# Where the sums, silus and splits of seven-product weight pairs stand in the engine queues

## The chip, the cores and the metric

One core of a Trainium2 chip runs the whole program in one launch. The metric is device time in microseconds (us); lower is better. All data is float32. Products run on TensorE (PE) as three float32r matmuls each: every operand is split into a high part and a remainder, and hi*hi, hi*lo and lo*hi are accumulated.

## The reference

A network of two blocks on 512 tokens of width 1024. What this change touches is the gated feed-forward layer of the second block, which is computed four times:

```python
def _swiglu(h, w_gu, w_down):
    gate, up = jnp.split(h @ w_gu, 2, axis=-1)
    return (jax.nn.silu(gate) * up) @ w_down

def second_block(x, ...):
    for l in range(DEPTH):                                  # DEPTH = 2
        x = _layer_norm(alpha * x + 0.5 * _swiglu(x, ffn_w_gu[l, 0], ffn_w_down[l, 0]), ...)
        mix = _token_mixers(x, ...)
        x = _layer_norm(alpha * x + mix, ...)
        x = _layer_norm(alpha * x + 0.5 * _swiglu(x, ffn_w_gu[l, 1], ffn_w_down[l, 1]), ...)
    return x
```

The hidden width is 2816, that is 22 chunks of 128 columns for the gate and 22 for the up half.

## The kernel before

A scheduling layer turns the program into one in-order queue per engine: PE, VectorE (DVE), ScalarE (ACT), GpSimd (POOL), and SyncE (SP), which issues every load. The scheduler may reorder, so the code's order is not quite the queue's; `tc.issue_after(ins)` keeps an instruction behind another one in its queue. An instruction that waits holds up everything behind it in its queue.

In `swiglu` (L1116) the hidden chunks are computed in three parts (8, 8 and 6 chunks), each followed by products with the down weights (`we`). The first four or five chunks of a layer go through `plain`. The others, 71 in all, go through `gated` (L1011): a chunk of gate weights and the chunk of up weights are a **pair**, and a 2 x 2 block product of the pair (gate and up weights split along the contraction, the operand split along contraction and tokens) is formed with seven products in place of eight. Seven-product pairs stand in twelve runs: one of 3 pairs, three of 4, four of 8 and four of 6.

A pair needs, in the order of the PE queue, the products named `11`, `12`, `p2`, `p1`, `p3`, `22` and `p4`, each of 12 matmuls on 256 columns. The products `22` and `p4` of a pair come one pair late: the loop in `swiglu` interleaves the generators, so that PE does 11(k), 12(k), 22(k-1), p2(k), p1(k), p4(k-1), p3(k), and then the next pair.

The weights come from `strassen_w` (L972). Two loads per pair, `ra` (tile wr, three buffers, L448) and `rb` (tile wr2, two buffers, L991); then four sums of 128 x 512 on POOL: p1 = a21 + a22 (L995), p2 = p1 + a11 (L996), p3 = a11 + a21 (L998), p4 = p2 + a12 (L999); then splits. A split is a copy on ACT that makes the high part (L472) and a subtraction on DVE that makes the remainder (L473). A pair has four weight splits: (11, 12) and (p2, p1), which share the buffers wh and wl, and (p3, p4), all of 128 x 1024, and (22) of 128 x 512.

The partial sums of the three products that share the PSUM tile R are copied out by ACT: e1 (L1028) after `11`, e2 (L1037) after `p2`, e3 (L1043) after `p3`. Since R goes on accumulating, PE may not start `p2` before e1, `p3` before e2, nor `22` before e3 is done. DVE adds what is left: g1 (L1032), g1 times up (L1051), g2 (L1054), n2 (L1045), the product with g2 (L1056). Two silus on ACT (L1023), and a split of the finished 128 x 512 chunk (tiles ph, pl).

Before a run of pairs the operand is prepared: `Strassen.combine` (L337) makes four sums of 128 x 256 on POOL for each of four operand blocks (L342 to L345) and splits them. That happens four times in the program, while `plain` runs.

Of the kernel before, what the change touches and what calls it, by code (L numbers as in the profile page):

```python
# [13 lines left out]
ALU = mybir.AluOpType  # L14
# [7 lines left out]
H = T // 2  # L22
# [280 lines left out]
class Strassen:  # L303
# [33 lines left out]
    def combine(self, j, x):  # L337
        nc, p = self.p.nc, self.p
        b11, b12, b21, b22 = (x[k][:, c] for k in (j, j + 4) for c in HALVES)
        raw = p.pool.tile([P, 2 * T], F32, tag="wc", name=p.nm("wc"), bufs=2)  # L340
        d, t3, t4, f = (raw[:, i * H : i * H + H] for i in range(4))
        nc.gpsimd.tensor_tensor(t3, b22, b12, op=ALU.subtract)  # L342
        nc.gpsimd.tensor_tensor(f, t3, b11, op=ALU.add)
        nc.gpsimd.tensor_tensor(d, b11, b12, op=ALU.subtract)
        nc.gpsimd.tensor_tensor(t4, f, b21, op=ALU.subtract)  # L345
        hi, lo = self.place(j, 3)
        nc.scalar.activation(hi, f, AF.Copy, scale=-1.0)
        nc.vector.scalar_tensor_tensor(
            out=lo, in0=f, scalar=-1.0, in1=hi.bitcast(F32), op0=ALU.mult, op1=ALU.subtract
        )  # L350
        for i, n in ((0, 2), (2, 1)) if j == 0 else ((0, 3),):
            p.split(raw[:, i * H : (i + n) * H], *self.place(j, i, n))


class Prog:
# [156 lines left out]

    def mac(self, W, X, cols=slice(0, T), tag=None, off=None):

# [452 lines left out]

        return X1, scale, X, finish

    def strassen_w(self, sa, sb, behind):  # L970


        nc = self.nc
        out = {}

        def put(names, src, tags, bufs=2, pool=None, behind=()):
            n = len(names) * 512
            hi, lo = ((pool or self.pool).tile([P, n], F32R, tag=t, name=self.nm(t), bufs=bufs) for t in tags)
            with ExitStack() as ctx:
                for ins in behind:  # L980
                    ctx.enter_context(self.tc.issue_after(ins))
                self.split(src, hi[:], lo[:])
            for i, name in enumerate(names):
                out[name] = [
                    (hi[:, c : c + P], lo[:, c : c + P]) for c in range(i * 512, i * 512 + 512, P)
                ]

        ra = self.raw(sa, 1024)
        put(("11", "12"), ra[:], ("wh", "wl"), pool=self.main)
        rb = self.pool.tile([P, 1024], F32, tag="wr2", name=self.nm("wr2"), bufs=2)  # L990
        nc.sync.dma_start(rb[:], sb)  # L991
        a11, a12, a21, a22 = ra[:, :512], ra[:, 512:], rb[:, :512], rb[:, 512:]
        c1, c2 = (self.pool.tile([P, 1024], F32, tag="wc", name=self.nm("wc"), bufs=2) for _ in range(2))
        p2, p1, p3, p4 = c1[:, :512], c1[:, 512:], c2[:, :512], c2[:, 512:]
        nc.gpsimd.tensor_tensor(p1, a21, a22, op=ALU.add)  # L995
        nc.gpsimd.tensor_tensor(p2, p1, a11, op=ALU.add)  # L996
        put(("p2", "p1"), c1[:], ("wh", "wl"), pool=self.main, behind=behind[0])
        nc.gpsimd.tensor_tensor(p3, a11, a21, op=ALU.add)  # L998
        nc.gpsimd.tensor_tensor(p4, p2, a12, op=ALU.add)  # L999
        put(("p3", "p4"), c2[:], ("wh2", "wl2"), behind=behind[1])  # L1000
        put(("22",), a22, ("wh3", "wl3"), 1)
        return out

    def prod(self, ps, W, X, start):

# [7 lines left out]
    def gated(self, X, srcs, mid, tags):  # L1013

        nc = self.nc
        tr, tq, tz = tags  # L1020
        gv, hv = self.scratch()
        g1, g2, e1, n2 = gv[:, :H], gv[:, H:], hv[:, :H], hv[:, H:]
        silu = lambda t: nc.scalar.activation(t, t, AF.Silu)  # L1023
        W = self.strassen_w(*srcs, self.behind)
        self.behind = behind = [[], []]
        R = self.pt(tag=next(tr))
        self.prod(R, W["11"], X["11"], True)
        nc.scalar.copy(e1, R[:, :H])  # L1028
        yield
        Z = self.pt(tag=next(tz))  # L1030
        self.prod(Z, W["12"], X["21"], True)
        behind[0].append(nc.vector.tensor_tensor(g1, e1, Z[:, :H], op=ALU.add).ins)  # L1032
        silu(g1)
        yield
        e2, e3 = (self.pool.tile([P, H], F32, tag="u", name=self.nm("u"), bufs=3)[:] for _ in range(2))
        self.prod(R, W["p2"], X["nf"], False)
        behind[0].append(nc.scalar.copy(e2, R[:, :H]).ins)  # L1037
        yield
        Q = self.pt(tag=next(tq))
        self.prod(Q, W["p1"], X["d"], True)  # L1040
        yield
        self.prod(R, W["p3"], X["t3"], False)
        behind[1].append(nc.scalar.copy(e3, R[:, :H]).ins)  # L1043
        behind[1].append(
            nc.vector.scalar_tensor_tensor(  # L1045
                out=n2, in0=e3, scalar=-1.0, in1=Q[:, :H], op0=ALU.mult, op1=ALU.subtract
            ).ins
        )
        yield
        self.prod(R, W["22"], X["t4"], False)  # L1050
        nc.vector.scalar_tensor_tensor(out=g1, in0=R[:, :H], scalar=-1.0, in1=g1, op0=ALU.mult, op1=ALU.mult)  # L1051
        yield
        self.prod(Q, W["p4"], X["22"], False)
        nc.vector.tensor_tensor(g2, e2, Q[:, :H], op=ALU.add)  # L1054
        silu(g2)
        nc.vector.tensor_tensor(g2, g2, n2, op=ALU.mult)  # L1056
        pair = self.xpair("m")
        self.split(gv[:], pair[0][:], pair[1][:])
        mid.append(pair)

    def plain(self, srcs, X, mid, normed):

        nc = self.nc
# [27 lines left out]
        else:  # L1091
            W = [self.weights(srcs[i], KC, None if i < 2 else ("wh2", "wl2")) for i in range(4)]
# [12 lines left out]
            for i in range(4, len(srcs)):  # L1105
                W = self.weights(srcs[i], KC)
# [4 lines left out]
                next(self.tail, None)  # L1111
        for _ in self.tail:
            pass
        self.behind = [self.last] * 2
        return X

    def swiglu(self, x, X, l, s, out=None, form=None, normed=None):


        nc, I = self.nc, self.I  # L1120
        wg = I[f"wg{l}{s}"]
        tags = cycle(("acc", "acc")), cycle(("s", "s")), cycle(("t", "t"))
        for a, b in PARTS:
            mid, j0 = [], a
            if a == 0:
                j0 = NPLAIN + (normed is not None)
                X = self.plain([wg[i * FC + j] for j in range(j0) for i in range(2)], X, mid, normed)
            before = iter(())
            for j in range(j0, b):
                g = self.gated(X, (wg[j], wg[FC + j]), mid, tags)  # L1130


                for one in (g, g, before, g, g, before, g):
                    next(one, None)
                before = g
            for _ in before:
                pass
            if b < FC:
                for nb in range(KC):
                    ps = self.proj(I[f"we{l}{s}"][nb][:, a * P : b * P], mid, b - a)  # L1140
                    nc.vector.scalar_tensor_tensor(
                        out=x[nb][:], in0=ps[:], scalar=0.5 / ALPHA, in1=x[nb][:], op0=ALU.mult, op1=ALU.add
                    )
# [959 lines left out]
```

## Time and profile before

| | |
|---|---|
| median of 3 runs | 3385.3 us (3382.5 to 3385.59) |
| the profiled execution | 3384.03 us, its span 3382.2 us |
| mean granted TensorE clock | 0.987 |
| PE busy | 3272.4 us (97%) |
| DVE busy | 2290.7 us (68%) |
| ACT busy | 1587.1 us (47%) |
| POOL busy | 875.3 us (26%) |

How to read it: the span runs from the first to the last instruction of the program. Busy times are unions of an engine's instructions. Matmuls are pipelined and each is shown longer than the distance to the next one, so PE's busy share says little of its idle time; the distance between the starts of the same product in successive pairs says more. DVE and ACT instructions that follow each other without a wait also overlap a little in the records. A timeline row has the start, the duration, the engine (SPq is SyncE's queue), the line, the operation, output and inputs, shapes, a count of merged instructions, and in brackets the idle time before it and what ended it.

### The profile page before, as it was taken

The page shows a single profiled execution, that of the slowest core. Times are in us where ns is not written, and L with a number is a line of the kernel's source. Part 1 is how long each engine was busy: PE and PEld are TensorE (multiplying, and loading weights), DVE is VectorE, ACT ScalarE, POOL GpSimd, SP SyncE. Part 2 cuts the span into 40 slices and gives each one's busy share as a digit, 9 for nine tenths or more (in the row PEclk, how much of TensorE's full clock was granted, in tenths as well). Part 3 has the DMA queues.
Part 4 walks back from the last instruction along what each step waited for, and adds up shares of the span by engine and source line. Part 5 has one row for each costly group of instructions (what it writes and reads, how often), then busy time and mean ns, then how long its engine had stood idle before and what let it go on. Part 6 is the DMA issues. An engine that isn't in the chain of part 4 may idle for free.

```text
span 3382.2 us, 47780 instructions
## 1 busy us (share of the span) xinstructions
PE 3272.4 (97%) x18386; PEld 2761.4 (82%) x18386; DVE 2290.7 (68%) x3708; ACT 1587.1 (47%) x3012; POOL 875.3 (26%) x635
## 2 busy tenths in 40 slices
PE   8999999998999999999999999999999999999998
PEld 6777888886788887899867798998998877789987
DVE  7866664648664647666677886668666767896666
ACT  6423443436442434344466653445443456754534
POOL 3111110114110104344200153444353410043534
PEclk9999999999999999999999999999999999999999
DMA  3321223231233323232312123222323322023232
GB/s 117 90 60 57 88 88 105 86 114 57 94 94 94 95 87 99 94 100 85 100 54 69 59 86 100 100 89 93 100 94 100 100 63 78 29 89 112 86 101 70
DMA packets 101109, 293.79 MB, mean 87 GB/s; under 512 B 20240, under 2 KB 26640, under 8 KB 100624
## 3 DMA queue, kind: packets, MB, share of 16 engines
q1 hardware_dynamic: 100880, 290.73, 27.4%
q8 instruction: 144, 2.36, 0.3%
q14 instruction: 85, 0.70, 0.1%
HBM read 280.20 MB, written 2.62 MB: 84 GB/s over the span
## 4 chain that ended last, share of the span: by engine, by line
PE 67%; DVE 13%; POOL 7%; issue 4%; ACT 4%; DMA 3%; SPq 0%; POOLq 0%; ACTq 0%; DVEq 0%
PE psacc L488 15%; PE psacc L490 14%; PE psacc L489 14%; PE pss L488 3%; DMA wr<-wg 3%; PE pss L490 3%; PE pss L489 3%; DVE wl L466 2%; PE pst L489 2%; PE pst L490 2%; PE pst L488 2%; POOL wc L996 2%; POOL wc L999 2%; POOL wc L995 1%; PE pst L1688 1%
## 5 line engine op out<-in xcount | busy, mean ns | idle before, releaser
L488 PE MATMUL psacc<-xh,wh 128*128 128x512 f32 (+1 forms) x1977 | 725.6, 369 | 36.1 <-ACT u L1043 12.1
L465 ACT ACTIVATE wh<-wr 128x512 fp32r<-128x512 f32 (+2 forms) x760 | 435.1, 611 | 643.0 <-PE psacc L489 379.2
L490 PE MATMUL psacc<-xh,wl 128*128 128x512 f32 (+1 forms) x1977 | 716.5, 363 | 12.1 <-DVE wl L466 9.6
L489 PE MATMUL psacc<-xl,wh 128*128 128x512 f32 (+1 forms) x1977 | 717.9, 364 | 2.9 <-DVE xl L590 1.5
L466 DVE TENSOR_TENSOR wl<-wr,wh 128x512 fp32r<-128x512 f32 (+2 forms) x760 | 581.1, 796 | 199.4 <-ACT wh L465 186.5
L488 PEld LDWEIGHTS psacc<-xh,wh 128*128 128x128 f32 x1977 | 377.4, 192 | 114.3 <-ACT u L1043 20.9
L490 PEld LDWEIGHTS psacc<-xh,wl 128*128 128x128 f32 x1977 | 377.5, 191 | 76.6 <-DVE wl L466 12.2
L489 PEld LDWEIGHTS psacc<-xl,wh 128*128 128x128 f32 x1977 | 376.9, 191 | 66.6 <-DVE xl L590 4.9
L488 PE MATMUL psacc<-ph,wh 128*128 128x512 f32 (+1 forms) x774 | 303.6, 393 | 5.5 <-DVE xs L473 2.2
L490 PE MATMUL psacc<-ph,wl 128*128 128x512 f32 (+1 forms) x774 | 303.6, 393 | 2.0 <-DVE wl L466 2.0
L489 PE MATMUL psacc<-pl,wh 128*128 128x512 f32 (+1 forms) x774 | 304.4, 393 | 0.4 <-DVE pl L939 0.3
L473 DVE TENSOR_TENSOR wl<-wc,wh 128x1024 fp32r<-128x1024 f32 x142 | 191.0, 1345 | 159.6 <-ACT wh L472 159.6
L472 ACT ACTIVATE wh<-wc 128x1024 fp32r<-128x1024 f32 x142 | 150.7, 1062 | 203.7 <-POOL wc L996 88.5
L653 POOL TENSOR_TENSOR cv<-cv,cv 128x512 f32<-128x512 f32 x44 | 57.3, 1303 | 542.7 <-DVE cv L644 517.6
L490 PE MATMUL psacc<-xs,wl 128*128 128x256 f32 (+1 forms) x671 | 194.6, 290 | 0.0
L488 PE MATMUL psacc<-xs,wh 128*128 128x256 f32 (+1 forms) x671 | 194.6, 290 | 0.0
L489 PE MATMUL psacc<-xs,wh 128*128 128x256 f32 (+1 forms) x671 | 194.1, 289 | 0.0
L473 DVE TENSOR_TENSOR wl<-wr,wh 128x512 fp32r<-128x512 f32 (+1 forms) x142 | 181.2, 1303 | 12.6 <-ACT wh L472 12.2
L488 PEld LDWEIGHTS psacc<-ph,wh 128*128 128x128 f32 x774 | 146.5, 189 | 39.2 <-issue 3.4
L490 PEld LDWEIGHTS psacc<-ph,wl 128*128 128x128 f32 x774 | 146.9, 190 | 34.4 <-DVE wl L466 2.4
L489 PEld LDWEIGHTS psacc<-pl,wh 128*128 128x128 f32 x774 | 146.9, 190 | 33.1 <-DVE pl L939 1.2
L995 POOL TENSOR_TENSOR wc<-wr 128x512 f32<-128x512 f32 x71 | 97.8, 1377 | 286.8 <-DMA wr<-wg 115.6
(546 smaller groups left out, 7508.3 us busy)
## 6 DMA issues: line engine op xcount, KB each, us to landing
wr<-wg SPq DMA_DIRECT2D x176, 512.0 KB, 3.8
wr<-wu SPq DMA_DIRECT2D x88, 512.0 KB, 3.6
wr<-we SPq DMA_DIRECT2D x64, 512.0 KB, 3.5
wr<-wd SPq DMA_DIRECT2D x32, 512.0 KB, 3.6
wr<-we SPq DMA_DIRECT2D x32, 384.0 KB, 3.1
wr<-wi SPq DMA_DIRECT2D x22, 512.0 KB, 3.6
wr<-w_ret SPq DMA_DIRECT2D x16, 512.0 KB, 3.6
wr<-wl_in SPq DMA_DIRECT2D x16, 512.0 KB, 3.6
```

Of the source, the lines that this page charges most:

```text
L465: one = nc.scalar.activation(hi[:, a:b], raw[:, a:b], AF.Copy)
L466: two = nc.vector.tensor_tensor(lo[:, a:b], raw[:, a:b], hi[:, a:b].bitcast(F32), op=ALU.subtract)
L472: nc.scalar.activation(hi, src, AF.Copy)
L473: nc.vector.tensor_tensor(lo, src, hi.bitcast(F32), op=ALU.subtract)
L488: nc.tensor.matmul(ps, wh, xh, start=start, stop=False, **kw)
L489: nc.tensor.matmul(ps, wh, xl, start=False, stop=False, **kw)
L490: nc.tensor.matmul(ps, wl, xh, start=False, stop=stop, **kw)
L653: nc.gpsimd.tensor_tensor(gate[:], gate[:], val[:], op=ALU.mult)
L995: nc.gpsimd.tensor_tensor(p1, a21, a22, op=ALU.add)
L996: nc.gpsimd.tensor_tensor(p2, p1, a11, op=ALU.add)
L999: nc.gpsimd.tensor_tensor(p4, p2, a12, op=ALU.add)
L1688: nc.tensor.transpose(pt[:, qb * P : (qb + 1) * P], t[:, kb * P - k0 : (kb + 1) * P - k0], self.ident)
```

## The change

The four weight sums of a pair and the four sums of `combine` go from POOL to DVE. `strassen_w` becomes a generator that `gated` drives, so that each split of weights is placed behind chosen instructions: (p2, p1) behind e2 and the g1 sum of the pair before, as it was; (p3, p4) behind e1 and the g1 sum of its own pair (before: behind e3 and n2 of the pair before); (22) behind e2 of its own pair (before: free). The silu of g1 goes behind e2, and the silu of g2, with the product and the split that follow it, behind e3 of the next pair, as an eighth step of the generator.

```diff
@@ combine
-        nc.gpsimd.tensor_tensor(t3, b22, b12, op=ALU.subtract)
-        nc.gpsimd.tensor_tensor(f, t3, b11, op=ALU.add)
-        nc.gpsimd.tensor_tensor(d, b11, b12, op=ALU.subtract)
-        nc.gpsimd.tensor_tensor(t4, f, b21, op=ALU.subtract)
+        nc.vector.tensor_tensor(t3, b22, b12, op=ALU.subtract)
+        nc.vector.tensor_tensor(f, t3, b11, op=ALU.add)
+        nc.vector.tensor_tensor(d, b11, b12, op=ALU.subtract)
+        nc.vector.tensor_tensor(t4, f, b21, op=ALU.subtract)
...
+    def queued(self, behind):
+
+        ctx = ExitStack()
+        for ins in behind:
+            ctx.enter_context(self.tc.issue_after(ins))
+        return ctx
...
@@ strassen_w
-        nc.gpsimd.tensor_tensor(p1, a21, a22, op=ALU.add)
-        nc.gpsimd.tensor_tensor(p2, p1, a11, op=ALU.add)
-        put(("p2", "p1"), c1[:], ("wh", "wl"), pool=self.main, behind=behind[0])
-        nc.gpsimd.tensor_tensor(p3, a11, a21, op=ALU.add)
-        nc.gpsimd.tensor_tensor(p4, p2, a12, op=ALU.add)
-        put(("p3", "p4"), c2[:], ("wh2", "wl2"), behind=behind[1])
-        put(("22",), a22, ("wh3", "wl3"), 1)
-        return out
+        nc.vector.tensor_tensor(p1, a21, a22, op=ALU.add)
+        nc.vector.tensor_tensor(p2, p1, a11, op=ALU.add)
+        behind = yield out
+        put(("p2", "p1"), c1[:], ("wh", "wl"), pool=self.main, behind=behind)
+        nc.vector.tensor_tensor(p3, a11, a21, op=ALU.add)
+        nc.vector.tensor_tensor(p4, p2, a12, op=ALU.add)
+        behind = yield
+        put(("p3", "p4"), c2[:], ("wh2", "wl2"), behind=behind)
+        behind = yield
+        put(("22",), a22, ("wh3", "wl3"), 1, behind=behind)
+        yield
@@ gated
+        weights = self.strassen_w(*srcs)
+        W = next(weights)
+        weights.send(self.behind)
...
-        behind[0].append(nc.vector.tensor_tensor(g1, e1, Z[:, :H], op=ALU.add).ins)
-        silu(g1)
+        add = nc.vector.tensor_tensor(g1, e1, Z[:, :H], op=ALU.add).ins
+        weights.send((one, add))
...
-        behind[0].append(nc.scalar.copy(e2, R[:, :H]).ins)
+        two = nc.scalar.copy(e2, R[:, :H]).ins
+        self.behind = (two, add)
+        with self.queued((two,)):
+            silu(g1)
+        weights.send((two,))
...
         nc.vector.tensor_tensor(g2, e2, Q[:, :H], op=ALU.add)
-        silu(g2)
+        yield
+
+        with self.queued((self.third,)):
+            silu(g2)
@@ swiglu
-                for one in (g, g, before, g, g, before, g):
+                for one in (g, g, before, g, g, before, g, before):
```

What the queues then hold. The order of the products in the PE queue does not move. The places are those of a pair in the middle of a run; a number behind a tile's name tells tiles apart, and L1038, L1047, L1057, L1032 of the changed file are the copies e1, e2, e3 and the silu.

ACT, from one e1 to the next, before (tile 12398/12399 is the pair k, wr_12531 and wr_2193_12537 feed the pair k+1, g_12267 is the pair k-1):

```order
L1028 COPY g_12399<-psacc_12426 128x256
L472 ACTIVATE wh_12533<-wr_12531 128x1024
L1023 ACTIVATE g_12398<-g_12398 128x256
L472 ACTIVATE wh_2179_12422<-wr_2172_12406 128x512
L1037 COPY u_12468<-psacc_12426 128x256
L472 ACTIVATE wh_12543<-wc_12539 128x1024
L1023 ACTIVATE g_12267<-g_12267 128x256
L1043 COPY u_12469<-psacc_12426 128x256
L472 ACTIVATE wh_2198_12549<-wc_12540 128x1024
L472 ACTIVATE ph_12511<-g_12267 128x512
```

and in the changed kernel:

```order
L1038 COPY g_12399<-psacc_12418 128x256
L472 ACTIVATE wh_2179_12446<-wc_12409 128x1024
L472 ACTIVATE wh_12533<-wr_12531 128x1024
L1047 COPY u_12463<-psacc_12418 128x256
L1032 ACTIVATE g_12398<-g_12398 128x256
L472 ACTIVATE wh_2183_12479<-wr_2172_12406 128x512
L472 ACTIVATE wh_12543<-wc_12539 128x1024
L1057 COPY u_12464<-psacc_12418 128x256
L1032 ACTIVATE g_12267<-g_12267 128x256
L472 ACTIVATE ph_12525<-g_12267 128x512
```

The split of (p3, p4) of the next pair (wh_2198) stood between e3 and e1; now that of the own pair (wh_2179, from wc_12409) stands behind e1. Both silus stand behind a copy: that of g1 behind e2, that of g2 behind e3.

DVE at the same place before, from n2 of the pair k to that of the pair k+1:

```order
L1045 SCALAR_TENSOR_TENSOR g_12399<-u_12469,pss_12483 128x256
L473 TENSOR_TENSOR wl_2199_12550<-wc_12540,wh_2198_12549 128x1024
L473 TENSOR_TENSOR pl_12512<-g_12267,ph_12511 128x512
L1032 TENSOR_TENSOR g_12529<-g_12530,pst_12571 128x256
L473 TENSOR_TENSOR wl_12665<-wr_12662,wh_12664 128x1024
L473 TENSOR_TENSOR wl_2201_12554<-wr_2193_12537,wh_2200_12553 128x512
L1051 SCALAR_TENSOR_TENSOR g_12398<-psacc_12426,g_12398 128x256
L473 TENSOR_TENSOR wl_12675<-wc_12670,wh_12674 128x1024
L1054 TENSOR_TENSOR g_12398<-u_12468,pss_12483 128x256
L1056 TENSOR_TENSOR g_12398<-g_12398,g_12399 128x256
L1045 SCALAR_TENSOR_TENSOR g_12530<-u_12600,pss_12614 128x256
```

and in the changed kernel, from the first sum for the pair k+2 (wr_12662, wr_2214) to the last split before g2 (here tile 12529/12530 is the pair k+1):

```order
L1001 TENSOR_TENSOR wc_12670<-wr_2214_12668 128x512
L1002 TENSOR_TENSOR wc_12670<-wc_12670,wr_12662 128x512
L473 TENSOR_TENSOR pl_12526<-g_12267,ph_12525 128x512
L1042 TENSOR_TENSOR g_12529<-g_12530,pst_12563 128x256
L473 TENSOR_TENSOR wl_2201_12578<-wc_12540,wh_2200_12577 128x1024
L1061 SCALAR_TENSOR_TENSOR g_12398<-psacc_12418,g_12398 128x256
L473 TENSOR_TENSOR wl_12665<-wr_12662,wh_12664 128x1024
L1005 TENSOR_TENSOR wc_12671<-wr_12662,wr_2214_12668 128x512
L473 TENSOR_TENSOR wl_2205_12611<-wr_2193_12537,wh_2204_12610 128x512
L1006 TENSOR_TENSOR wc_12671<-wc_12670,wr_12662 128x512
L473 TENSOR_TENSOR wl_12675<-wc_12670,wh_12674 128x1024
```

L1001, L1002, L1005 and L1006 are p1, p2, p3 and p4, which the POOL queue held. Three instructions of 128 x 256 follow (g2, n2, the product), and then L1001 of the next pair.

SP in the middle of a run of 8, before (L448 loads ra, L991 rb; wr_11342 and wr_2014 belong to one pair, wr_11473 and wr_2035 to the next):

```order
L448 DMA wr_11473<-wg 128x1024
L991 DMA wr_1993_11217<-wg 128x1024
L448 DMA wr_11604<-wg 128x1024
L991 DMA wr_2014_11348<-wg 128x1024
L448 DMA wr_11735<-wg 128x1024
L991 DMA wr_2035_11479<-wg 128x1024
```

and in the changed kernel (L997 loads rb):

```order
L448 DMA wr_11342<-wg 128x1024
L997 DMA wr_1993_11217<-wg 128x1024
L448 DMA wr_11473<-wg 128x1024
L997 DMA wr_2014_11348<-wg 128x1024
L448 DMA wr_11604<-wg 128x1024
L997 DMA wr_2035_11479<-wg 128x1024
```

With wr_11342 as the ra of a pair p, wr_2014 is its rb. It stood behind wr_11604, the ra of the pair p+2, whose buffer is free when p4 of the pair p-1 is done; now it stands behind wr_11473, the ra of the pair p+1, whose buffer is free when p4 of the pair p-2 is done. The buffer of the rb itself is free when the (22) split of the pair p-2 is done, before and after. In the last pairs of a run loads of `we` (L462) take the place of the ra, with the same waits.

## Rows read from the trace of the kernel before

**Rows 1.** The page's busy times: us, share of the span, instructions.
```profile
PE 3272.4 (97%) x18386; PEld 2761.4 (82%) x18386; DVE 2290.7 (68%) x3708; ACT 1587.1 (47%) x3012; POOL 875.3 (26%) x635
```

**Rows 2.** Windows over the runs of 8 and 6 pairs: stretch, length, busy us (instructions).
```profile
core 0: us, PE busy (x) PEld busy (x) DVE busy (x) ACT busy (x) POOL busy (x), PEclk, DMA share, GB/s
...
2465.66:2546.80 81.14, 77.97 (x649) 76.57 (x648) 57.14 (x75) 44.19 (x76) 43.35 (x27) 1.00 0.26 94
2594.98:2653.93 58.95, 57.44 (x482) 56.63 (x481) 42.95 (x56) 32.71 (x57) 29.84 (x18) 1.00 0.24 73
...
sum 559.27, PE 542.64 PEld 534.12 DVE 398.08 ACT 307.38 POOL 292.49; mean PE 67.83 PEld 66.77 DVE 49.76 ACT 38.42 POOL 36.56
```

**Rows 3.** Timeline of PE: first matmul of product 12 in five pairs of one run.
```profile
2474.14 0.28 PE L488 MATMUL pst<-xh,wh 128*128 128x256 f32 x1
...
2483.99 0.28 PE L488 MATMUL pst<-xh,wh 128*128 128x256 f32 x1
...
2514.06 0.28 PE L488 MATMUL pst<-xh,wh 128*128 128x256 f32 x1
...
2526.04 0.28 PE L488 MATMUL pst<-xh,wh 128*128 128x256 f32 x1
...
2537.09 0.28 PE L488 MATMUL pst<-xh,wh 128*128 128x256 f32 x1
```

**Rows 4.** Timeline of ACT in a late pair of that run.
```profile
2524.50 1.06 ACT L472 ACTIVATE wh<-wc 128x1024 fp32r<-128x1024 f32 x1 [3.06 <-POOL wc L996]
2527.19 0.42 ACT L1023 ACTIVATE g<-g 128x256 f32<-128x256 f32 x1 [1.62 <-DVE g L1054]
2527.51 0.35 ACT L1043 COPY u<-psacc 128x256 f32<-128x256 f32 x1
2528.01 1.06 ACT L472 ACTIVATE wh<-wc 128x1024 fp32r<-128x1024 f32 x1
2528.97 0.61 ACT L472 ACTIVATE ph<-g 128x512 fp32r<-128x512 f32 x1
2529.49 0.35 ACT L1028 COPY g<-psacc 128x256 f32<-128x256 f32 x1
```

**Rows 5.** Timeline of SP's queue: issues of loads in those pairs.
```profile
2516.96 0.33 SPq L462 DMA_DIRECT2D wr<-we  x1
2517.38 0.38 SPq L991 DMA_DIRECT2D wr<-wg  x1
2528.00 0.33 SPq L462 DMA_DIRECT2D wr<-we  x1
```

**Rows 6.** Timeline of POOL: first and last of the four sums of a pair.
```profile
2521.80 1.31 POOL L995 TENSOR_TENSOR wc<-wr 128x512 f32<-128x512 f32 x1 [4.87 <-DMA wr<-wg]
...
2525.68 2.29 POOL L999 TENSOR_TENSOR wc<-wc,wr 128x512 f32<-128x512 f32 x1
```

**Rows 7.** Tile wr in that run: from issue to landing of its loads.
```profile
DMA to landing us min/median/max: 3.4/3.6/5.2
```

**Rows 8.** Timeline of DVE in a late pair.
```profile
2518.06 1.22 DVE L473 TENSOR_TENSOR wl<-wc,wh 128x1024 fp32r<-128x1024 f32 x1 [0.52 <-ACT wh L472]
2519.20 0.68 DVE L473 TENSOR_TENSOR pl<-g,ph 128x512 fp32r<-128x512 f32 x1
2519.80 0.41 DVE L1032 TENSOR_TENSOR g<-g,pst 128x256 f32<-128x256 f32 x1
2520.13 1.82 DVE L473 TENSOR_TENSOR wl<-wr,wh 128x1024 fp32r<-128x1024 f32 x2
```

**Rows 9.** Window over the run of 3 pairs, in the columns of rows 2.
```profile
1343.71:1378.85 35.14, 30.72 (x228) 30.09 (x229) 27.77 (x31) 17.90 (x30) 19.32 (x11) 0.90 0.31 96
```

**Rows 10.** Timeline at the start of that run: DVE, then ACT.
```profile
1336.71 2.31 DVE L466 TENSOR_TENSOR wl<-wr,wh 128x512 fp32r<-128x512 f32 x2
...
1347.17 2.00 ACT L472 ACTIVATE wh<-wc 128x1024 fp32r<-128x1024 f32 x2 [2.06 <-POOL wc L999]
```

**Rows 11.** Groups of PE: products of `plain` that waited for a weight split.
```profile
L490 PE MATMUL pss<-xh,wl 128*128 128x256 f32 x475 | 133.2, 281 | 1.8 <-DVE wl L466 1.7
```

More of the change, by code (lines that the diff above doesn't have):

```diff
@@ L968, in normed, with strassen_w @@
         return X1, scale, X, finish
-    def strassen_w(self, sa, sb, behind):
+    def queued(self, behind):
[3 more added lines that the diff above has]
+        return ctx
+    def strassen_w(self, sa, sb):
         nc = self.nc
@@ L978, in put @@
             hi, lo = ((pool or self.pool).tile([P, n], F32R, tag=t, name=self.nm(t), bufs=bufs) for t in tags)
-            with ExitStack() as ctx:
-                for ins in behind:
-                    ctx.enter_context(self.tc.issue_after(ins))
+            with self.queued(behind):
                 self.split(src, hi[:], lo[:])
@@ L1023, in gated @@
         silu = lambda t: nc.scalar.activation(t, t, AF.Silu)
-        W = self.strassen_w(*srcs, self.behind)
-        self.behind = behind = [[], []]
+        weights = self.strassen_w(*srcs)
+        W = next(weights)
+        weights.send(self.behind)
         R = self.pt(tag=next(tr))
         self.prod(R, W["11"], X["11"], True)
-        nc.scalar.copy(e1, R[:, :H])
+        one = nc.scalar.copy(e1, R[:, :H]).ins
         yield
@@ L1042, in gated @@
         self.prod(R, W["p3"], X["t3"], False)
[L1043 to L1048, printed above, removed]
+        self.third = nc.scalar.copy(e3, R[:, :H]).ins
+        nc.vector.scalar_tensor_tensor(out=n2, in0=e3, scalar=-1.0, in1=Q[:, :H], op0=ALU.mult, op1=ALU.subtract)
         yield
@@ L1113, in plain @@
             pass
-        self.behind = [self.last] * 2
+        self.behind = self.last
         return X
```

## The prediction

> **What bounds the kernel now.** I read the page's busy times first. PE is busy 97% of the span, DVE 68%, POOL 26% [rows 1]. That alone would say that nothing done on POOL or DVE can matter. But matmuls overlap in the records, so I went to stages: windows over the runs of seven-product pairs, and in one of them the timelines of PE, ACT, POOL, SP and DVE.
>
> In the first pairs of a run the same product starts 9.85 us apart: 2474.14 and 2483.99 [rows 3]. A pair has 84 matmuls, so that is 0.1173 us a matmul, PE without a stall. Late in the run the distances are 11.98 and 11.05 (2514.06, 2526.04, 2537.09). The reader is to see that PE has a pace of its own and loses it.
>
> How much in all: the eight runs of 8 and 6 pairs last 559.27 us in sum [rows 2]. A run of 8 has 54 products between these borders and one of 6 has 40, so 4 x 94 = 376 products of 12 matmuls at 0.1173 us, 529.1 us. PE loses **30.2 us** there, some 5 us in a run of 8 and 2 in a run of 6.
>
> Who sets the pace of 11.05: SP issues the rb load at 2517.38; POOL's p1 starts at 2521.80, when it has landed, 4.42 later; p1 to p4 last until 2527.97, 6.17; SP issues the next load of its queue at 2528.00, and the next rb 0.42 behind it, as it did at 2516.96 and 2517.38 [rows 5, 6]. 0.42 + 4.42 + 6.17 + 0.03 = 11.04: a **circle of load and POOL sums**, since the rb load is queued behind a load that waits for p4 of the pair before. ACT shows what comes of it: the high part of (p2, p1) waits 3.06 us for POOL, the silu of g2 1.62 us for DVE, then e3 at 2527.51, and e1 only at 2529.49, behind two splits [rows 4]. PE waits for both copies in that pair.
>
> **The change, part by part.** *The circle.* POOL leaves it. On DVE a 128 x 512 instruction takes 0.68 us and the next starts 0.60 after it; 128 x 1024 takes 1.22 and 1.14; 128 x 256 takes 0.41 and 0.33 (starts 2518.06, 2519.20, 2519.80, 2520.13) [rows 8]. The trace has no sum of this kind on DVE; the nearest row is the subtraction of 128 x 512, with the same two inputs in SBUF, 0.68. POOL needs 1.31 to 2.29 for one [rows 6]; I take 0.68, and keep 1.31 as the far end.
>
> The new order ties rb to the (22) split of the pair two back, no longer to p4 of the pair before. From that split's end to the next one's: issue 0.03, landing 3.6 (the median; 3.4 to 5.2 [rows 7]), start 0.1, then DVE's queue: p1 0.71 (p2 waits for its result), p2 0.60, the finished chunk's split 0.60, g1 0.33, (p3, p4) 1.14, g1 times up 0.33, (11, 12) 1.14, p3 0.60, (22) 0.68, together 6.13. The new circle is **9.86 us**, against PE's 9.85. I take the median of 3.6 since the rb load now follows no other load by 0.42; with 4.42 the circle is 10.68, with 5.2 it is 11.46.
>
> *DVE's load.* Three instructions of 1.14, six of 0.60, five of 0.33: 8.67 us of each 9.85, 88%. It is under PE's pace, with little to spare. What is queued behind a wait of p1 for its load is all of the above; who waits for that in the end is ACT (silus, splits) and, two queues later, PE.
>
> *Copies.* Count from the start of product 11, with 1.41 us a product. e3 of the pair before: 0.2 to 0.55. Silu of g2 to 0.9, product on DVE to 1.35, high part of the chunk to 2.0, e1 to 2.3. PE wants e3 at 2.8 (product 22) and e1 at 4.2 (p2): 2 us to spare for each. The (p3, p4) split behind e1 ends near 4.7 on DVE and is wanted at 8.4; (22) ends near 7.8 and is wanted in the next pair. So both stalls go. What is late next is e1, if DVE falls over 2 us behind.
>
> *The sum for the runs.* All 30.2 us would be the best end. The circle of 9.86 leaves no reserve for a slow load, so I leave 0.6 us a run: **-25**.
>
> *The run of 3 pairs.* [...] ACT waited 2.06 us there for p4, with the splits that PE wanted behind it, and two DVE splits of 128 x 512 beside POOL took 2.31 where 1.28 is their price alone [rows 10, 8]. The (p3, p4) split now stands behind e1, and POOL is quiet. But DVE is busiest there and gets the sums of `combine` too: 16 x 0.33 = 5.3 us at each of four places. Ends: -8.4, and +5.3 if nothing of the load is hidden. I take half the loss, **-4**, as both named waits vanish.
>
> *The other three `combine` places.* Waits of PE in `plain` for a weight split are 1.7 us in sum [rows 11]. The added 5.3 us are paid for by splits that no longer run beside POOL (1.03 saved on the pair of splits in rows 10). Ends: -1.7, and +15.9 if all of it came on the path. I take **-1**, near the row.
>
> Silus and splits behind copies cost no instruction. Loads keep their number; the SP queue is passed only by rb, one place earlier.
>
> Sum: -25 - 4 - 1 = -30. The profiled execution, 3384.0 us, becomes 3354.0; it lies 1.3 below the median of 3385.3, so I forecast **3355 us**.
>
> [...] The rows show the next instruction starting 0.08 before the end of the one before [rows 8]. [...]
>
> **The rivals.** (a) *The load sets the pace, in part.* Landing takes 4.42 as in rows 5 and 6. The circle of 10.68 loses 0.83 us a pair; the first two pairs of a run have their rb early, and 2 us are to spare. A run of 8 loses 6 x 0.83 - 2 = 3.0, one of 6 loses 1.3, together 17, so 13 are won: 3372. For it: the ra load still follows rb 0.6 later. Against: the second load of two is the late one now.
>
> (b) *Slower: DVE stands still for the load.* The same circle at the longest landing, 5.2. It loses 1.61 a pair: 4 x (6 x 1.61 - 2) + 4 x (4 x 1.61 - 2) = 48.4, and three runs of 4 lose 1.2 each: 52 against 30.2, +22: 3407. The point from which it decides is a loss of 1.155 us a pair, that is a landing with its waits of 4.75 us. POOL could wait for a load with nobody behind it; DVE has everything behind it.
>
> (c) *No difference.* The copies are in time, but PE waits for splits instead, as DVE, 88% full, hands out one late whenever two wanted ones meet; or the orders of the queues change while the weights come no sooner. Some 30 us lost as before: 3385.
>
> (d) *A DVE instruction holds the next one off.* If each did so for half its own length, the 14 (9.79 us of durations) would take 14.7 us a pair; 71 x 4.85 = 344, less 30 lost before: 3698. Rows 8 speak against it. [...]
>
> **How the numbers follow.** Forecast 0.64, (a) 0.15, (c) 0.10, (b) 0.10, (d) 0.01. A measurement of this kernel tells some 0.2% from no change, 6.8 us. Faster by more: forecast and (a), 0.79. Within: 0.10. Slower: 0.11. The range begins where all of the three losses go, 30.2 + 8.4 + 1.7 = 40, with some 4 us for a clock that does not fall: 3341. It reaches over (a) to the middle of (c), 3386; left out are (b), (d), half of (c) and a little of the forecast, under 2 in 10.
>
> **What would show it.** Right: windows over the eight runs of 529 to 536 us in sum; the same product 9.85 apart to the end of a run; PE's waits for e1 and e3 gone; p1 on DVE waiting under 0.5 us for its load; DVE at 85 to 90% in a run of 8. Rival (a) or (b) shows as p1 waiting over 1 us for wr and the late pairs 10.7 or 11.5 apart. (c) shows as PE waiting for DVE's wl. The forecast is wrong if the runs keep over 15 us of their loss, or if the stretches with `combine` grow by over 3 us each.

## The result and the profile after

The changed kernel takes **3335.0 us** (median of 4 runs, 3331.6 to 3337.4) against 3383.9 us, a ratio of 0.9858 with an interval of 0.9845 to 0.987: 48.9 us faster. I had said 3355, with a range that began at 3341. The sign was right, the gain is larger than any I had allowed for. The profiled execution of the changed kernel took 3336.26 us, 47.8 less than that of the kernel before; the parts below add up to these 47.8.

The page's busy times answer to [rows 1]:

```profile
PE 3252.0 (98%) x18386; PEld 2754.7 (83%) x18386; DVE 2330.3 (70%) x4056; ACT 1584.8 (48%) x3012; POOL 350.4 (11%) x287
```

DVE got 348 more instructions and only 39.6 us more busy time. The sums alone are 284 of 0.69 us and 64 of 0.41, together 222 us. Busy time counts records that overlap once; the sum of all durations went from 2490.3 to 2559.5 us, 69 more. So some 150 us of DVE's old work vanished. The two largest groups of DVE that became shorter hold 96 of them, first before, then after; behind the first bar stand busy us and mean ns of one, behind the second the idle time ahead of them.

```profile
L473 DVE TENSOR_TENSOR wl<-wr,wh 128x512 fp32r<-128x512 f32 (+1 forms) x142 | 181.2, 1303 | 12.6 <-ACT wh L472 12.2
L466 DVE TENSOR_TENSOR wl<-wr,wh 128x512 fp32r<-128x512 f32 (+2 forms) x760 | 581.1, 796 | 199.4 <-ACT wh L465 186.5
```

```profile
L466 DVE TENSOR_TENSOR wl<-wr,wh 128x512 fp32r<-128x512 f32 (+2 forms) x760 | 532.7, 731 | 193.9 <-ACT wh L465 179.9
L473 DVE TENSOR_TENSOR wl<-wr,wh 128x512 fp32r<-128x512 f32 (+1 forms) x142 | 133.9, 949 | 18.3 <-ACT wh L472 18.2
```

The same splits, as many and as large, are shorter with POOL quiet. This was in the profile of before, and I used it for one stretch only.

Windows over the runs of pairs, in the columns of [rows 2]: two of the eight runs, and their sum.

```profile
2436.27:2512.30 76.03, 76.03 (x649) 76.03 (x648) 68.67 (x106) 45.75 (x78) 0.00 (x0) 1.00 0.32 103
2560.04:2616.38 56.34, 56.34 (x481) 56.33 (x480) 49.83 (x77) 33.54 (x58) 0.00 (x0) 1.00 0.26 85
...
sum 529.49, PE 529.49 PEld 529.46 DVE 474.41 ACT 317.51 POOL 0.00; mean PE 66.19 PEld 66.18 DVE 59.30 ACT 39.69 POOL 0.00
```

559.27 us became 529.49, against 529.1 for PE without a stall. PE, whose records overlap, is busy through every window. The timeline of PE, first matmul of product 12 in late pairs, answers to [rows 3]: 9.85 apart to the end.

```profile
2484.14 0.28 PE L488 MATMUL pst<-xh,wh 128*128 128x256 f32 x1
...
2493.99 0.28 PE L488 MATMUL pst<-xh,wh 128*128 128x256 f32 x1
...
2503.83 0.28 PE L488 MATMUL pst<-xh,wh 128*128 128x256 f32 x1
```

Timelines of ACT, DVE and SP in the same pairs answer to [rows 4 to 6]:

```profile
2492.86 0.37 ACT L1057 COPY u<-psacc 128x256 f32<-128x256 f32 x1 [1.89 <-PE psacc L490]
...
2494.60 0.35 ACT L1038 COPY g<-psacc 128x256 f32<-128x256 f32 x1
```

```profile
2495.46 0.69 DVE L1001 TENSOR_TENSOR wc<-wr 128x512 f32<-128x512 f32 x1 [1.43 <-DMA wr<-wg]
2496.19 0.69 DVE L1002 TENSOR_TENSOR wc<-wc,wr 128x512 f32<-128x512 f32 x1
2496.80 0.69 DVE L473 TENSOR_TENSOR pl<-g,ph 128x512 fp32r<-128x512 f32 x1
```

```profile
2490.80 0.33 SPq L997 DMA_DIRECT2D wr<-wg  x1
...
2501.65 0.33 SPq L997 DMA_DIRECT2D wr<-wg  x1
```

e3 (L1057) now waits for PE, not PE for it. It is done at 2493.23 and PE's product `22` begins at 2495.35; e1 (L1038) is done at 2494.95 and `p2` begins at 2496.76. So 2.1 and 1.8 us are to spare, near the 2 that I had worked out. p1 (L1001) waits 1.43 us for its load here, with all of DVE's queue behind it, and the two rb loads are 10.85 apart; PE does not feel it.

### The profile page after: what moved, and what is told of

It is laid out like the page before. It is cut to its first block, busy times and chain, and to the rows that moved or that the text cites. A ratio compares the mean times of both kernels' runs of the same rounds, so it can differ in the third digit from the quotient of the medians.

```text
span 3334.4 us, 47631 instructions
## 1 busy us (share of the span) xinstructions
PE 3252.0 (98%) x18386; PEld 2754.7 (83%) x18386; DVE 2330.3 (70%) x4056; ACT 1584.8 (48%) x3012; POOL 350.4 (11%) x287
## 4 chain that ended last, share of the span: by engine, by line
PE 78%; issue 9%; DVE 9%; ACT 2%; POOL 1%; DMA 0%; SPq 0%; ACTq 0%; DVEq 0%; POOLq 0%
PE psacc L488 17%; PE psacc L489 16%; PE psacc L490 16%; PE pss L488 4%; PE pss L489 4%; PE pss L490 4%; PE pst L489 3%; PE pst L488 3%; PE pst L490 3%; DVE wl L466 1%; PE pso L490 1%; PE pso L488 1%; PE pso L489 1%; DVE cv L669 1%; DVE h L875 1%
## 5 line engine op out<-in xcount | busy, mean ns | idle before, releaser
L466 DVE TENSOR_TENSOR wl<-wr,wh 128x512 fp32r<-128x512 f32 (+2 forms) x760 | 532.7, 731 | 193.9 <-ACT wh L465 179.9
L473 DVE TENSOR_TENSOR wl<-wc,wh 128x1024 fp32r<-128x1024 f32 x142 | 173.0, 1218 | 3.5 <-ACT wh L472 3.4
L473 DVE TENSOR_TENSOR wl<-wr,wh 128x512 fp32r<-128x512 f32 (+1 forms) x142 | 133.9, 949 | 18.3 <-ACT wh L472 18.2
L472 ACT ACTIVATE wh<-wr 128x512 fp32r<-128x512 f32 (+1 forms) x142 | 118.8, 837 | 48.1 <-PE pst L489 26.7
L488 PE MATMUL pss<-xh,wh 128*128 128x256 f32 x475 | 133.5, 281 | 1.3 <-ACT wh L472 1.3
```

Of the source, the lines that this page charges most:

```text
L466: two = nc.vector.tensor_tensor(lo[:, a:b], raw[:, a:b], hi[:, a:b].bitcast(F32), op=ALU.subtract)
L472: nc.scalar.activation(hi, src, AF.Copy)
L473: nc.vector.tensor_tensor(lo, src, hi.bitcast(F32), op=ALU.subtract)
L488: nc.tensor.matmul(ps, wh, xh, start=start, stop=False, **kw)
```

## The experiments

For each kernel the table has the ratio to the kernel before (95% interval), the sum of the eight runs of 8 and 6 pairs, DVE's busy time in them, and the distance of late pairs in the runs of 8. Sums and distances are from windows and timelines as above.

| kernel | ratio | eight runs, us | DVE busy | late pairs |
|---|---|---|---|---|
| before | 1 | 559.3 | 398.1 | 10.4 to 13.7 |
| changed | 0.9858 (0.9845, 0.987) | 529.5 | 474.4 | 9.85 |
| E1 early rb load alone | 0.9989 (0.9979, 0.9998) | 559.0 | 489.0 | 10.35 and 11.7 by turns |
| E2 pair sums alone | 0.9901 (0.9885, 0.9917) | 531.3 | 447.3 | 9.85 |
| E3 new places alone | 1.0116 (1.01, 1.0132) | 592.8 | 401.9 | 11.5 |
| E4 combine alone | 0.9978 (0.9968, 0.9987) | 560.2 | 397.5 | 10.4 to 13.9 |
| E5 changed, combine on POOL | 0.9875 (0.9859, 0.9892) | 529.6 | 474.6 | 9.85 |
| E6 changed, POOL kept busy | 1.0357 (1.0341, 1.0372) | 647.4 | 599.9 | 13.0, some up to 15.3 |
| E7 changed, 1 more sum | 0.9871 (0.9857, 0.9886) | 530.8 | 488.1 | 9.85, once 10.7 |
| E8 changed, 3 more sums | 0.9881 (0.9866, 0.9895) | 531.0 | 518.8 | 9.85 |
| E9 changed, rb load held back | 0.988 (0.9863, 0.9896) | 532.3 | 469.2 | 9.85 to 10.5 |
| E10 all sums, old places | 0.9877 (0.9862, 0.9891) | 531.7 | 446.6 | 9.85 |
| E12 new places, early rb load | 1.0013 (1.0004, 1.0023) | 567.1 | 510.6 | 10.5 to 11.4 |

**E1.** The theory of my prediction was the circle, so I broke it and did nothing else.

```diff
@@ raw and load_split
-        self.nc.sync.dma_start(t[:, :n], src)
+        with self.behind_rb():
+            self.nc.sync.dma_start(t[:, :n], src)
...
+    def behind_rb(self):
+        self.ahead += 1
+        left = [ins for k, ins in enumerate(self.rbs) if k + 3 <= self.ahead]
+        return self.tc.issue_after(left[-1]) if left else nullcontext()
@@ strassen_w
-        nc.sync.dma_start(rb[:], sb)
+        self.rbs, self.ahead = (*self.rbs, nc.sync.dma_start(rb[:], sb).ins), len(self.rbs) + 1
```

> The kernel before with one thing moved: in SP's queue the rb load of a pair stands one place earlier, ahead of the ra load that waits for p4 (the place it has in the changed kernel). Sums stay on POOL, the queues of ACT, DVE, POOL and PE are word for word those of before. Theory (a circle of rb load and POOL sums, closed by the rb load standing behind a load that waits for p4 of the pair before): this alone breaks the circle, POOL's four sums need 6.17 us of 9.85, so the late pairs come 9.85 to 10.1 apart, the eight runs of 8 and 6 pairs last 530 to 540 us in sum in place of 559.3, and the time is 3355 to 3365. Rival A (the copies behind splits and silus on ACT set the late pairs' pace): the runs stay at 555 or more, the time at 3380 to 3385. Rival B (POOL's sums themselves are too slow beside DVE, wherever the load stands): late pairs at 10.5 or more, 3372 or more.

3378.1 against 3381.3 us, and the runs last 559.0 as before. Late pairs come 10.35 and 11.7 apart by turns, 11.0 on average. What took the circle's place stands in DVE's timeline of a late pair, with POOL's beside it:

```profile
2506.91 1.78 DVE L482 TENSOR_TENSOR wl<-wc,wh 128x1024 fp32r<-128x1024 f32 x1 [0.47 <-ACT wh L481]
2508.62 1.77 DVE L482 TENSOR_TENSOR pl<-g,ph 128x512 fp32r<-128x512 f32 x1
2510.31 0.41 DVE L1041 TENSOR_TENSOR g<-g,pst 128x256 f32<-128x256 f32 x1
2510.64 3.69 DVE L482 TENSOR_TENSOR wl<-wr,wh 128x1024 fp32r<-128x1024 f32 x2
```

```profile
2506.31 1.30 POOL L1004 TENSOR_TENSOR wc<-wr 128x512 f32<-128x512 f32 x1 [2.52 <-DMA wr<-wg]
2507.69 2.15 POOL L1005 TENSOR_TENSOR wc<-wc,wr 128x512 f32<-128x512 f32 x1
2509.80 1.75 POOL L1007 TENSOR_TENSOR wc<-wr,wr 128x512 f32<-128x512 f32 x1
2511.51 2.27 POOL L1008 TENSOR_TENSOR wc<-wc,wr 128x512 f32<-128x512 f32 x1
```

In the kernel before these splits took 1.22, 0.68 and 1.82 us [rows 8]. The early load starts POOL's sums early, and they run beside DVE's splits: 3.5 us more for DVE in this pair, and sums of 1.3 grow to 2.2. PE now waits for DVE:

```profile
2536.80 0.39 PE L497 MATMUL psacc<-xh,wh 128*128 128x256 f32 x1 [1.02 <-DVE g L1060]
```

The circle had kept three of the four sums in time in which DVE waited for POOL anyway. Rival B holds: POOL's sums beside DVE's splits limit the pair wherever the load stands.

**E2.** The reverse: the four sums of a pair on DVE, nothing else changed by hand.

```diff
-        nc.gpsimd.tensor_tensor(p1, a21, a22, op=ALU.add)
+        nc.vector.tensor_tensor(p1, a21, a22, op=ALU.add)
```

and so for p2, p3 and p4.

> The kernel before with only the four sums of a pair on DVE; the sums of combine stay on POOL, silus and splits stand where they stood, except where the scheduler places the rb load one place earlier by itself. Theory of the circle: the circle is gone, the eight runs last 530 to 538 us in sum, the time is 3354 to 3362. Rival A (order of ACT's queue): the copies e1 and e3 still stand behind splits of 1.06 us, the runs stay at 548 or more, the time at 3374 or more.

3347.4 us; the runs fall to 531.3, as expected, and the time is 7 us below the range I gave. The scheduler moved the rb load one place earlier by itself. Against E1, where that load stands early too and the sums are on POOL, it is 27.7 us in the runs for the engine on which the sums run.

**E3.** All sums on POOL, silus and splits in the places of the change (every `nc.vector` of the change's two blocks of sums back to `nc.gpsimd`).

> The changed kernel with all eight kinds of sums back on POOL: silus and splits stand behind the copies as in the change, and the scheduler puts the rb load back behind the ra load that waits for p4. Theory of the circle: the circle of 11.04 us is there again, late pairs 10.9 to 11.1 apart, the runs at 553 us or more in sum, the time 3375 to 3388. Rival A (order of ACT's queue): the copies are on time, the runs fall to 529 to 540, the time to 3355 to 3365.

3418.7 us. The circle's theory had the direction, but its 3375 to 3388 and its 11.1 were too low. In the runs of 8 PE loses its pace two pairs earlier than in the kernel before, and the late pairs are 11.5 apart and not 11.0. PE waits for e1 in each late pair, and the circle is there again, in SP's queue and on POOL:

```profile
2538.20 0.39 PE L488 MATMUL psacc<-xh,wh 128*128 128x256 f32 x1 [1.41 <-ACT g L1038]
```

```profile
2525.88 0.38 SPq L997 DMA_DIRECT2D wr<-wg  x1
2536.97 0.33 SPq L462 DMA_DIRECT2D wr<-we  x1
2537.39 0.38 SPq L997 DMA_DIRECT2D wr<-wg  x1
```

```profile
2530.50 1.58 POOL L1001 TENSOR_TENSOR wc<-wr 128x512 f32<-128x512 f32 x1 [5.07 <-DMA wr<-wg]
...
2534.65 2.29 POOL L1006 TENSOR_TENSOR wc<-wc,wr 128x512 f32<-128x512 f32 x1
```

From the issue of rb to p1 4.62, the four sums 6.44, the next issue of the queue 0.03 later and the next rb 0.42 behind it: 11.51, the distance of late pairs.

**E12** put E1's early load on top of E3, to tell a circle from ACT's queue.

> The new places of silus and splits with all sums on POOL, as in the third run (3418.7 us, late pairs 11.51 apart), and now the rb load one place earlier in SP's queue. If the circle of load and POOL sums set that pace of 11.51, it falls to the 11.0 that DVE beside POOL allowed in the first run: late pairs 10.3 to 11.2 apart, 3375 to 3395. If it did not, and ACT's queue behind the late split of (p2, p1) did: 11.4 or more, 3410 or more.

3387.3 us, runs 567.1, late pairs 10.5 to 11.4. The circle did set E3's pace: 25.7 us of the runs went with it. What is left is again DVE beside POOL, busy for 510.6 of 567.1 us.

**E4 and E5** take `combine` apart from the pairs.

```diff
-        nc.gpsimd.tensor_tensor(t3, b22, b12, op=ALU.subtract)
+        nc.vector.tensor_tensor(t3, b22, b12, op=ALU.subtract)
```

and its three others; E4 in the kernel before, E5 the reverse in the changed one.

> The kernel before with only the sums of combine on DVE. Theory: the run of 3 pairs and its entry give 4 to 8 us, since no DVE split runs beside POOL there and the splits no longer wait for POOL; the other three places give 0 to 3; the eight runs stay at 557 to 561 us. Time 3373 to 3381. Rival: the 5.3 us of sums come on the path at each of the four places: 3390 to 3405.

3371.8 against 3381.3 us, a little under the range I gave: 9.4 won by the medians and 4 to 11 by the interval; the runs are unchanged. In the profiled executions the run of 3 and the 64 us ahead of it are 4.3 us shorter.

> The changed kernel with the sums of combine back on POOL; the pair sums stay on DVE, the queues of the pairs as in the change. If the two moves add up (combine alone took 9.4 us from the kernel before), this gives back 6 to 10 us: 3341 to 3346, all of it at the four places of combine and in the run of 3 pairs, the eight runs of 8 and 6 pairs unchanged at 529 to 531 us. Rival: with the pair sums gone from POOL it no longer matters where combine runs: 3333 to 3338.

3341.7 us. Against the changed kernel's 3335.0, of another session, that is 6 us given back, but the intervals of the two ratios overlap. The traces settle one place: the run of 3 and the 64 us ahead of it are 3.8 us shorter than in the kernel before, where the changed kernel has 9.5 and the same kernel again (E13) 8.2. So `combine` on DVE is worth 4 to 6 us there; what it is worth at the other three places stays open.

**E6** is the test of the collisions: nobody waits for POOL any more, but it works.

```diff
+        again = self.bct()
+        nc.gpsimd.tensor_tensor(again[:], a21, a22, op=ALU.add)
+        for _ in range(3):
+            nc.gpsimd.tensor_tensor(again[:], again[:], again[:], op=ALU.add)
```

> The changed kernel, and POOL makes four more sums of 128 x 512 per pair, the first from rb, into a buffer that nobody reads: nobody waits for POOL, but POOL is busy beside DVE as in the kernel before. Theory after the first four runs (DVE and POOL stretch each other: in the run with the early rb load, splits of 0.68 took 1.77 beside POOL, some 3.5 us a pair): DVE's work of 8.67 us a pair grows to 12 or more against PE's 9.85, late pairs 11.5 to 13 us apart, some 2.3 us lost in each of 71 pairs less 2 us of reserve in each of 12 runs, time 3430 to 3540. Rival (only the waits for POOL's results and for the rb load cost time, the stretching is hidden): 3333 to 3342, runs at 529 to 533 us.

3503.2 us, 168 more than the changed kernel; the orders of PE, ACT, DVE and SP are the same. DVE at the head of a late pair, and POOL:

```profile
2592.05 1.81 DVE L1001 TENSOR_TENSOR wc<-wr 128x512 f32<-128x512 f32 x1 [0.74 <-DMA wr<-wg]
2593.89 1.41 DVE L1002 TENSOR_TENSOR wc<-wc,wr 128x512 f32<-128x512 f32 x1
2595.23 1.52 DVE L473 TENSOR_TENSOR pl<-g,ph 128x512 fp32r<-128x512 f32 x1
2596.68 0.41 DVE L1046 TENSOR_TENSOR g<-g,pst 128x256 f32<-128x256 f32 x1
2597.01 1.73 DVE L473 TENSOR_TENSOR wl<-wc,wh 128x1024 fp32r<-128x1024 f32 x1
2598.66 0.41 DVE L1065 SCALAR_TENSOR_TENSOR g<-psacc,g 128x256 f32<-128x256 f32 x1
```

```profile
2592.03 1.29 POOL L1004 TENSOR_TENSOR bc<-wr 128x512 f32<-128x512 f32 x1 [7.45 <-DMA wr<-wg]
2593.39 4.26 POOL L1006 TENSOR_TENSOR bc<-bc 128x512 f32<-128x512 f32 x3
```

While POOL works, four DVE instructions take 6.5 us in place of 3.3. The one at 2596.68 reads one operand from PSUM (pst) and keeps its 0.41. PE's late pairs are 13 us apart.

**E7 and E8** ask how much room DVE has: one or three more sums of 128 x 512 per pair, into a buffer that nobody reads.

```diff
+        again = self.bct()
+        for _ in range(3):
+            nc.vector.tensor_tensor(again[:], a11, a12, op=ALU.add)
```

> The changed kernel, and DVE makes one more sum of 128 x 512 per pair into a buffer that nobody reads: 0.60 us, DVE at 9.27 of 9.85 us a pair. Theory (DVE has 1.18 us of room in a pair): late pairs stay 9.85 apart, the eight runs 529 to 533 us, time 3334 to 3341. Rival (the change has used DVE's room up, because of its waits for rb): 0.5 us or more lost in each late pair, time 3355 or more.

3339.6 us, runs 530.8: as expected, but under about half the load I meant. The scheduler put only 32 of the 56 extra sums inside the windows of the eight runs.

> As the run before, with three more sums per pair: DVE at 10.47 us of 9.85. Theory: DVE sets the pace, late pairs 10.4 to 10.6 apart, 0.62 us lost in each of 71 pairs less some 2 us of reserve in each of 12 runs, time 3350 to 3372. Rival (a DVE instruction costs its whole duration of 0.68 and more behind another): 10.8 or more apart, time 3385 or more.

3343.0 us and late pairs 9.85 apart: the expectation fell, since the load on DVE was not the one I meant. As nobody reads these sums, the scheduler put only 96 of 168 inside the windows of the eight runs, 1.7 a pair. What it shows is still of use:

```profile
sum 531.03, PE 531.03 PEld 529.96 DVE 518.81 ACT 317.01 POOL 0.00; mean PE 66.38 PEld 66.24 DVE 64.85 ACT 39.63 POOL 0.00
```

```profile
2489.27 0.69 DVE L1009 TENSOR_TENSOR wc<-wc,wr 128x512 f32<-128x512 f32 x1
2489.87 0.69 DVE L1005 TENSOR_TENSOR bc<-wr 128x512 f32<-128x512 f32 x1
```

DVE is busy for 98% of the runs, its instructions start 0.60 apart, and PE loses 1.5 us more in all eight. More sums on DVE than fit into PE's pace were not tried.

**E9** closed the other half of the question on the load: rb held back behind the ra load of the pair after next.

```diff
-        nc.sync.dma_start(rb[:], sb)
+        with self.queued((self.last_ra,)):
+            nc.sync.dma_start(rb[:], sb)
```

(ra loads are issued two pairs ahead, so that there is one to stand behind.)

> The changed kernel with the rb load of a pair held back in SP's queue behind the ra load of the pair after next, which waits for p4 of the pair before, as in the kernel before; the sums stay on DVE, where the scheduler now puts p1 and p2 some four instructions further back. Theory (what hurt was POOL: its sums are slow, and they stretch DVE's splits; the load's place is of little worth by itself): the circle is now 0.42 + 4.42 of the load and 3.4 of DVE from p1 to p4 in the new order, 8.3 us, under PE's 9.85: runs at 529 to 535 us, time 3333 to 3345. Rival (the load's place is what the change lives from): with the 6.1 us that p1 to p4 span in the changed kernel the circle would be 11 us, runs at 550 or more, time 3358 or more.

3341.1 us, runs 532.3, within the expectation. With the sums on DVE the load's place is worth under 3 us in the runs. The edit also moves the ra loads and, by the scheduler, p1 and p2 in DVE's queue, so it does not test the place alone.

**E10, E13, E14.** All sums on DVE, silus and splits where they stood before (the edits of E2 and E4 together); then the changed kernel and this one again, side by side on one chip.

> The kernel before with all eight kinds of sums on DVE and nothing else: silus and splits stand where they stood. Against the changed kernel this shows what the places behind the copies are worth once POOL is quiet. Theory: under 5 us, since the runs with the pair sums alone on DVE lost only 1.7 us against PE's pace: 3335 to 3341. Rival (the places are needed, as the step from pair sums alone to pair sums with the new places, 8 us, says): 3342 to 3347.

> The changed kernel as it is, on the same chip as the next run. Expected 0.985 to 0.988 of the kernel before, the eight runs at 529 to 530 us.

> All sums on DVE, silus and splits where they stood before, beside the changed kernel on the same chip. If the new places are worth what the traces show (2.2 us in the eight runs, some 0.5 at the borders), this is 1 to 5 us slower than the changed kernel; if they are worth what the ratios of different sessions show, 5 to 9 us.

E10 took 3340.7 us, at the upper end of what the theory gave. Side by side it was 3336.1 for the changed kernel (0.9862, 0.9842 to 0.9883) and 3340.5 for the sums alone (0.9876, 0.9855 to 0.9897). The runs differ by 1.7 to 2.2 us: with the old places the fourth pair of a run comes 0.2 late, in one run 0.5. So the new places are worth some 2 us in the runs and 4 in the medians, whose intervals overlap.

**E11** tried one chunk less in `plain` (`NPLAIN = 3`), the only version that might have beaten the change.

> The changed kernel with three chunks in place of four in plain (four in place of five in the first), so one more seven-product pair in each of the four layers. [...] Expected: 3332 to 3338 if combine is hidden under three chunks; if its 5.3 us on DVE and the splits behind them are not, 3340 to 3355.

3347.6 us, 0.99 (0.9885 to 0.9914): the second case. No run shows what a chunk of `plain` costs more than a pair, on which the 3332 to 3338 rest. In the trace of before matmuls of 128 x 512 start 0.233 us apart (1382.47 to 1426.34, 188 distances); by that the 48 of a chunk are 11.2 us, an estimate, against 9.85 for a pair.

## Why the prediction was right in sign and short in size

The sum said -30 and the profiled executions differ by -47.8. Two steps failed. The term "I leave 0.6 us a run" left a loss in the runs that did not come (4.8 us). And the sum had three terms only, with "The range begins where all of the three losses go, 30.2 + 8.4 + 1.7 = 40" as its end; stretches outside the three, priced at nothing, gave 5.9 us, and the last of the three 4.2 where its end was 1.7. The first step alone would have left the time inside the range; the second, with 1.9 us of the run of 3 and some chance, took it out.

*The runs: -25 forecast, -29.8 measured.* The step was "the circle of 9.86 leaves no reserve for a slow load, so I leave 0.6 us a run". The load was slower than the 3.6 I took; tile wr in the run of 8 shown above:

```profile
DMA to landing us min/median/max: 3.4/4.1/5.2
```

p1 did wait for its load, as rivals (a) and (b) had it: 31.1 us in 51 of 71 pairs, 0.6 on average and 1.86 at the worst, not the 0.5 I allowed. But PE lost only 0.4 us of 30.2. I read it so that the 2 us to spare, which I had worked out for e1 and e3 and put only into the rivals, took the waits up; 31.1 us of them over 71 pairs are also less than the 1.18 us a pair that DVE had left.

*The mechanism behind that term was half of it.* "A circle of load and POOL sums" describes the pace that the trace shows, and E3 with E12 show that such a circle sets a pace. But breaking it alone frees nothing: E1 opened it and won 0.2 us in the runs, E9 closed it again with sums on DVE and lost under 3 us. A second limit lay at the same 11 us: POOL and DVE stretch each other (E1, E6). Moving the sums off POOL takes both away, so the sign and most of the runs' size came out for a reason half of which I had named for `combine` alone. For E1 the same reasoning forecast 3355 to 3365, and that was wrong.

*The run of 3 pairs: -4 forecast, -5.9 measured*, from [rows 9] to this window, with the granted clock at 1.00 and not 0.90:

```profile
1338.14:1367.37 29.23, 27.50 (x229) 26.94 (x228) 27.83 (x43) 17.18 (x30) 0.00 (x0) 1.00 0.38 110
```

"Half the loss" was too little; it was a choice between two ends, and 2.5 of the 8.4 us are left: this window and that of [rows 9], each less 26.7 us, which is 228 matmuls at the 0.1173 us of a pair without a stall. The two moves are needed together: pair sums alone (E2) won 1.5 us there, combine alone (E4) 1.0, both without the new places (E10) 6.1.

*Places I had priced at nothing.* The 64 us ahead of that run, in which `combine` works, became 3.6 us shorter; I had charged `combine` to the run of 3 alone. E4, E10 and E14 win 3.3 to 3.6 there too, E2, E3 and E5, with `combine` on POOL, 1.2 or less. PE's one wait for a split of `plain` in that stretch is gone, and its mean granted clock is 0.97 in place of 0.93:

```profile
1337.93 0.50 PE L490 MATMUL pss<-x,wl 128*128 128x512 f32 x1 [1.09 <-DVE wl L466]
```

The other three places of `combine`, with the runs of 4 behind them and the stretches between the layers ahead of two of them, gave 4.2 and not 1. PE's waits there for a split of `plain`, 0.7, 0.2 and 0.7 us, are gone; those I had priced. Half of the 4.2 is one spot, ahead of the second of these runs, though the run behind it grew by 1.1. PE waited there for a norm's small instruction on POOL; the rows are of PE and of POOL, before:

```profile
2344.03 0.43 PE L562 MATMUL pso<-cbt,f 128*128 128x128 f32 x2 [2.15 <-POOL f L546]
```

```profile
2341.30 1.83 POOL L875 TENSOR_TENSOR h<-h,bc 128x256 f32<-128x256 f32 x2 [11.68 <-ACT bc L872]
2343.10 0.87 POOL L546 TENSOR_TENSOR f<-f,mhalf 128x2 f32<-128x2 f32 x1
```

and POOL after:

```profile
2312.16 0.70 POOL L546 TENSOR_TENSOR f<-f,mhalf 128x2 f32<-128x2 f32 x1 [11.08 <-DVE f L867]
2312.83 2.58 POOL L875 TENSOR_TENSOR h<-h,bc 128x256 f32<-128x256 f32 x3
```

L546 stood behind two products that waited for another copy; now it stands ahead of them. The scheduler did so in the kernels with the new places (E3 and E5 win the same 2.2 us there) and not in those without (E4, E10). It is a side effect, not an effect of the sums, and a step that I could have read in POOL's queue, at a place I did not look at. The products with `we` behind the runs gave another 2.3 us. They did so in E3 as well (2.3) and in E1 (1.7), with the sums on POOL, so the sums are not the cause; it stays open.

*Chance.* The first 1280 us, which the change does not touch, were 2.0 us shorter; 3.0 us shorter at the one spot of the clock shown in the last section. In the profiled executions of the other kernels the same stretch differs from that of before by -5.0 (E4) to +1.7 us (E6).

The stretches between the layers, some 360 us each, differ by up to 5 us in the same way, so part of the 4.2 may be chance too: the same kernel again (E13) won 8.6 at these places.

In sum -29.8 - 5.9 - 3.6 - 4.2 - 2.3 - 2.0 = -47.8. Against the end of 40.3 us, the runs and the run of 3 stayed 2.9 inside their ends; the other three places went 2.5 over theirs, the two stretches that I had not priced added 5.9 and chance 2.0. The margin of 4 us, meant for the clock, did not cover that.

*What held.* Both stalls at e1 and e3 are gone; DVE is at 90% in the eight runs (474.4 of 529.5) where I had 88%; rival (d) is out, since E8 ran DVE at 98% with starts 0.60 apart; rival (c) is out, as PE waits for no split in the runs.

## What to carry to other kernels

Before costing an instruction that moves from POOL to DVE, compare the durations of DVE's instructions with two inputs in SBUF while POOL works and while it rests (here 1.77 and 0.68 us for a split of 128 x 512): the stretch that goes may pay for most of what comes (here some 150 of 222 us). A loop that matches the measured pace is not yet the cause: break it at its cheapest edge, here one place in SP's queue, and see whether the pace goes; a second limit may stand right behind it. Where PE has time to spare for one late input, it can also cover the waits of the engines that feed it (here p1 waited 31.1 us and PE lost 0.4), so such a reserve belongs into the forecast and not only into the rivals.

## What the hardware showed that I had not expected

DVE and POOL stretch each other, in the rows of E1 and E6 by up to 1.1 us: splits of 128 x 512 took 0.68 us alone and 1.77 beside POOL, POOL's sums 1.30 and 2.27 (E1), in E6 1.81 for a sum of 0.69. The instructions with an operand in PSUM that ran meanwhile kept their 0.41 (2510.31 in E1, 2596.68 in E6). In E1's first rows the one that starts while the other engine is at work pays, in turn: when the split at 2506.91, p2 at 2507.69, the split at 2508.62 and p3 at 2509.80 start, the other engine has 0.70, 1.00, 1.22 and 0.59 us left, and they take 0.56, 0.85, 1.09 and 0.45 longer than alone (1.22, 1.30, 0.68, 1.30).

The granted clock dips at different places in executions of the same work. Windows over one stretch of the mixer, before and then after, whose instructions are the same:

```profile
270.00:290.00 20.00, 19.76 (x81) 13.62 (x80) 10.85 (x25) 4.38 (x12) 2.02 (x2) 0.83 0.08 26
```

```profile
270.00:290.00 20.00, 19.76 (x95) 13.82 (x94) 12.43 (x28) 6.20 (x15) 2.31 (x3) 1.00 0.16 52
```

PE did 14 more matmuls in the same 20 us at a granted clock of 1.00 than in the window at 0.83. In the latter the clock was 0.50 from 272 to 278: nine matmuls of 128 x 512 from 274.68 to 278.09 start 0.43 us apart, five from 278.68 to 279.61 0.23. The same matmul comes 0.5 us earlier than before at the start of this window and 3.5 us earlier at 280: one such dip is worth 3.0 us, more than several of the terms above.
